# Splitting the last 1 KB of columns off the last store of a 2x2 max-unpool

## Chip, cores, metric

One core of one Trainium2 chip. The metric is device time in microseconds (us) of one execution, as the median of several; "span" is the time from the first to the last instruction in the profile, about 1.3 us shorter. Differences here are a few hundredths to a few tenths of a us in 71.5, so most experiments were timed in five rounds (those with 4 KB columns in three) beside the kernel before, each call on one chip, and the text quotes intervals. SBUF is the memory in which the kernel allocates its tiles, HBM the one that holds its inputs and its output (the profile counts 12.58 MB read from it and 16.78 MB written).

## The reference

```python
# x: 16 x 64 x 32 x 32 float32, indices: int32 in 0..3, kernel_size = 2
for b, c, i, j in every input element:          # loops shortened
    idx = indices[b, c, i, j]
    output[b, c, 2*i + idx // 2, 2*j + idx % 2] = x[b, c, i, j]   # the rest is zero
```

The launch passes the indices as 64-bit integers, so the kernel reads 8.4 MB of indices and 4.2 MB of x, and writes 16.8 MB.

## The kernel before

The 1024 images lie eight to an SBUF row (partition), 128 rows. Four loads are issued at once; VectorE computes each output position as `(index == position) * x`; the output goes out in four stores (NG = 4) of 128 rows x 32 KB. All transfers are issued by SyncE.

```python
        program.first(nc.sync.dma_start(out=x_t, in_=x_v).then_inc(x_in, 16))
        ...                                                   # three loads of idx, VectorE work
        for g in range(NG):
            nc.sync.wait_ge(made, g + 1)
            nc.sync.dma_start(out=out_v[g], in_=out_t[g]).then_inc(
                stored if g else stored_0, 16
            )
        nc.sync.sem_inc(made, -NG)
        program.last(
            nc.sync.wait_ge(stored, 16 * (NG - 1)).then_inc(stored, -16 * (NG - 1))
        )
```

The kernel ends when the last wait sees every increment of the last three stores: in the profile the last of them lands at 70.31 us and the span ends at 70.35.

Of the kernel before, what the change touches and what calls it, by code (L numbers as in the profile page):

```python
# [1 line left out]

# [4 lines left out]

P = 128
F32 = mybir.dt.float32
I32 = mybir.dt.int32  # L10


class Program:




    def __init__(self, nc):
        self.nc = nc
        self.block = nc.main_func.blocks[0]  # L20
        self.kernel_block = nc.cur_bb.bb.name

    def __enter__(self):
        ins = self.block.instructions
        self.branches = [i for i in ins if "Branch" in type(i).__name__]
        n = len(ins) - len(self.branches)
        assert all("Branch" in type(ins[k]).__name__ for k in range(n, len(ins)))
        del ins[n:]
        self.nc.switch_bb(self.block.name, parent=None)
        self.symbolic = self.nc._always_lower_symbolic_ap  # L30
        self.nc._always_lower_symbolic_ap = False
        return self

    def first(self, made):
        ins = self.block.instructions
        assert ins[len(ins) - 1].name == made.ins.name
        moved = ins.pop()
        at = next(
            k
            for k, i in enumerate(ins)  # L40
            if i.engine == moved.engine and isinstance(i, mybir.InstDrain)
        )
        ins.insert(at, moved)

    def last(self, made):


        def move(nc):
            ins = self.block.instructions
            at = next(k for k, i in enumerate(ins) if i.name == made.ins.name)  # L50
            nc.main_func.blocks[-1].instructions.append(ins.pop(at))

        self.nc.at_finalize(move)

    def __exit__(self, kind, *_):
        self.nc._always_lower_symbolic_ap = self.symbolic
        if kind is None:
            for b in self.branches:
                self.block.instructions.append(b)
            self.nc.switch_bb(self.kernel_block, parent=None)  # L60


@with_exitstack
def kernel(
    ctx: ExitStack,
    tc: tile.TileContext,
    x: bass.AP,
    indices: bass.AP,
    kernel_size: bass.AP,
    out: bass.AP,  # L70
):
    nc = tc.nc
    assert kernel_size == 2

    B, C, H, W = x.shape
    n_img = B * C
    T = n_img // P
    assert T * P == n_img and C % T == 0

    G = 2  # L80
    NG = T // G
    FIRST = 3
    N = H * W
    x_v = x.rearrange("b (ch t) h w -> (b ch) (t h w)", t=T)
    idx_v = indices.rearrange("b (ch t) h w -> (b ch) (t h w)", t=T).bitcast(I32)
    out_v = out.rearrange("b (ch g t) oh ow -> g (b ch) (t oh ow)", g=NG, t=G)

    x_t = nc.alloc_sbuf_tensor("x_t", [P, T * N], F32).ap()
    idx_t = nc.alloc_sbuf_tensor("idx_t", [P, T * 2 * N], I32).ap()
    out_t = [  # L90
        nc.alloc_sbuf_tensor(f"out_t{g}", [P, G * 4 * N], F32).ap()
        for g in range(NG - 1)
    ]
    out_t.append(out_t[0])

    x_in = nc.alloc_semaphore("x_in")
    idx_in = [nc.alloc_semaphore(f"idx_in{g}") for g in range(2)]
    made = nc.alloc_semaphore("made")
    stored_0 = nc.alloc_semaphore("stored_0")
    stored = nc.alloc_semaphore("stored")  # L100

    x_c = x_t.rearrange("p (t i j) -> p t i j", t=T, j=W)
    idx_c = idx_t.rearrange("p (t i j two) -> p t i j two", t=T, j=W, two=2)[
        :, :, :, :, 0
    ]
    cut = FIRST * 2 * N

    with Program(nc) as program:
        for part in (slice(0, 2 * N), slice(2 * N, cut)):
            program.first(  # L110
                nc.sync.dma_start(out=idx_t[:, part], in_=idx_v[:, part]).then_inc(
                    idx_in[0], 16
                )
            )
        program.first(nc.sync.dma_start(out=x_t, in_=x_v).then_inc(x_in, 16))
        program.first(
            nc.sync.dma_start(out=idx_t[:, cut:], in_=idx_v[:, cut:]).then_inc(
                idx_in[1], 16
            )
        )  # L120

        nc.vector.wait_ge(x_in, 16).then_inc(x_in, -16)
        for t in range(T):
            g, k = t // G, t % G
            if t in (0, FIRST):
                half = int(t == FIRST)
                n_in = 16 if half else 32
                nc.vector.wait_ge(idx_in[half], n_in).then_inc(idx_in[half], -n_in)  # L128


            if k == 1 and t != FIRST and g:
                continue
            n = 1 if k == 1 or t + 1 == FIRST or not g else 2
            if g == NG - 1:
                nc.vector.wait_ge(stored_0, 16).then_inc(stored_0, -16)
            o_c = out_t[g].rearrange(
                "p (m i two j wo) -> p m i two j wo", m=G, two=2, wo=2, j=W
            )

            parts = (slice(0, H // 2), slice(H // 2, H)) if t == 0 else (slice(0, H),)  # L140
            for rows in parts:
                for pidx in range(4):
                    op = nc.vector.scalar_tensor_tensor(  # L143
                        out=o_c[:, k : k + n, rows, pidx // 2, :, pidx % 2],
                        in0=idx_c[:, t : t + n, rows],
                        scalar=pidx,
                        in1=x_c[:, t : t + n, rows],
                        op0=mybir.AluOpType.is_equal,
                        op1=mybir.AluOpType.mult,
                    )  # L150
            if k + n == G:
                op.then_inc(made, 1)

        for g in range(NG):
            nc.sync.wait_ge(made, g + 1)
            nc.sync.dma_start(out=out_v[g], in_=out_t[g]).then_inc(
                stored if g else stored_0, 16
            )
        nc.sync.sem_inc(made, -NG)
        program.last(  # L160
            nc.sync.wait_ge(stored, 16 * (NG - 1)).then_inc(stored, -16 * (NG - 1))
        )


# [1 line left out]
_INS = ['x', 'indices', 'kernel_size']  # L166
_OUTS = [((16, 64, 64, 64), 'float32')]

_NUMBERS = {'kernel_size': 2}


# [26 lines left out]
```

## Time and profile before

| | before |
|---|---|
| median of 3 runs | 71.46 us (71.41 to 71.53) |
| the execution that was profiled | 71.67 us, span 70.3 us |
| VectorE busy | 36.1 us, 51% |
| DMA packets fill | 97.4% of 16 engines |

### The profile page before, as it was taken

The page shows a single profiled execution, that of the slowest core. Times are in us where ns is not written, and L with a number is a line of the kernel's source. Part 1 is how long each engine was busy: PE and PEld are TensorE (multiplying, and loading weights), DVE is VectorE, ACT ScalarE, POOL GpSimd, SP SyncE. Part 2 cuts the span into 40 slices and gives each one's busy share as a digit, 9 for nine tenths or more (in the row PEclk, how much of TensorE's full clock was granted, in tenths as well). Part 3 has the DMA queues.
Part 4 walks back from the last instruction along what each step waited for, and adds up shares of the span by engine and source line. Part 5 has one row for each costly group of instructions (what it writes and reads, how often), then busy time and mean ns, then how long its engine had stood idle before and what let it go on. Part 6 is the DMA issues. An engine that isn't in the chain of part 4 may idle for free.

```text
span 70.3 us, 81 instructions
## 1 busy us (share of the span) xinstructions
DVE 36.1 (51%) x28; POOL 0.2 (0%) x4
## 2 busy tenths in 40 slices
DVE  0000000000089999999999999999999700000000
POOL 1000000000000000000000000000000000000000
DMA  4999996979988999869898998979698989989790
GB/s 84 405 443 438 456 559 298 578 317 540 429 373 373 466 582 443 373 298 540 354 540 354 429 466 373 522 317 578 298 540 354 522 373 410 484 354 540 317 540 37
DMA packets 1152, 29.36 MB, mean 417 GB/s; under 512 B 128, under 2 KB 128, under 8 KB 128
## 3 DMA queue, kind: packets, MB, share of 16 engines
q1 hardware_dynamic: 1152, 29.36, 97.4%
HBM read 12.58 MB, written 16.78 MB: 417 GB/s over the span
## 4 chain that ended last, share of the span: by engine, by line
DVE 45%; DVEq 5%; issue 2%
DVE out_t L143 45%; DVEq L193 5%
## 5 line engine op out<-in xcount | busy, mean ns | idle before, releaser
L143 DVE SCALAR_TENSOR_TENSOR out_t<-idx_t,x_t 128x1024 f32<-128x1024 int32 (+2 forms) x28 | 36.1, 1370 | 19.6 <-DVEq L128 19.6
L179 POOL MEMSET const-bfloat16-1.0<- 128x1 bf16 x1 | 0.1, 102 | 0.0
L179 POOL MEMSET const-uint8-127<- 128x1 uint8 x1 | 0.1, 102 | 0.0
L179 POOL MEMSET const-float32-0.0<- 128x1 f32 x1 | 0.1, 99 | 0.2 <-issue 0.2
L179 POOL MEMSET const-float32-1.0<- 128x1 f32 x1 | 0.1, 99 | 0.0
## 6 DMA issues: line engine op xcount, KB each, us to landing
out_dram<-out_t SPq DMA_DIRECT2D x4, 4096.0 KB, 13.2
idx_t<-in_indices_dram SPq DMA_DIRECT2D x1, 5120.0 KB, 30.1
x_t<-in_x_dram SPq DMA_DIRECT2D x1, 4096.0 KB, 18.5
idx_t<-in_indices_dram SPq DMA_DIRECT2D x1, 2048.0 KB, 9.3
idx_t<-in_indices_dram SPq DMA_DIRECT2D x1, 1024.0 KB, 4.8
```

The lines of the kernel that those rows point to most:

```text
L143: op = nc.vector.scalar_tensor_tensor(out=o_c[:, k : k + n, rows, pidx // 2, :, pidx % 2], in0=idx_c[:, t : t + n, rows], scalar=pidx, in1 ...
L179: nc = _bacc.Bacc("TRN2", target_bir_lowering=False, num_devices=1)
L193: with _tile.TileContext(nc) as tc:
```

## The change

The intent: if one of the 16 DMA engines ends later than the rest, take some of its share of the last store. The store is cut into 31 KB columns for all 128 rows, the last 1 KB of 120 rows, and the last 1 KB of the other 8 rows. The 120 rows fall to 15 engines, eight rows each, and the 8 rows to eight of them, one each; the sixteenth has 8 KB less to move. Here and in the recorded texts "engine 15" is a name for the engine that gets none of the small rows, or none of a store of 120 rows, "0 to 7" for the eight with nine of them and "8 to 14" for the seven with eight.

```diff
+    REST = 256
...
+        rest = slice(G * 4 * N - REST, None)
+        pieces = (
+            (slice(0, P), slice(0, rest.start)),
+            (slice(0, 15 * P // 16), rest),
+            (slice(15 * P // 16, P), rest),
+        )
         for g in range(NG):
             nc.sync.wait_ge(made, g + 1)
-            nc.sync.dma_start(out=out_v[g], in_=out_t[g]).then_inc(
-                stored if g else stored_0, 16
-            )
+            for rows, cols in pieces if g == NG - 1 else ((slice(0, P), slice(None)),):
+                nc.sync.dma_start(
+                    out=out_v[g][rows, cols], in_=out_t[g][rows, cols]
+                ).then_inc(stored if g else stored_0, 16)
...                                    # the last wait counts 16 * (NG - 2 + len(pieces))
```

More of the change, by code (lines that the diff above doesn't have):

```diff
@@ L152 @@
                 op.then_inc(made, 1)
+        rest = slice(G * 4 * N - REST, None)
[4 more added lines that the diff above has]
+        )
         for g in range(NG):
             nc.sync.wait_ge(made, g + 1)
-            nc.sync.dma_start(out=out_v[g], in_=out_t[g]).then_inc(
-                stored if g else stored_0, 16
-            )
+            for rows, cols in pieces if g == NG - 1 else ((slice(0, P), slice(None)),):
+                nc.sync.dma_start(
+                    out=out_v[g][rows, cols], in_=out_t[g][rows, cols]
+                ).then_inc(stored if g else stored_0, 16)
         nc.sync.sem_inc(made, -NG)
-        program.last(
-            nc.sync.wait_ge(stored, 16 * (NG - 1)).then_inc(stored, -16 * (NG - 1))
-        )
+        n_stored = 16 * (NG - 2 + len(pieces))
+        program.last(nc.sync.wait_ge(stored, n_stored).then_inc(stored, -n_stored))
 _INS = ['x', 'indices', 'kernel_size']
```

## The prediction

Where the prediction rests on something that no trace or run here shows, the passage is cut and the cut is marked. The forecast's sum came to a gain of 0.06 us, 71.40 us in all. The split of the small rows over the engines, on which the 300, 46 and 95 ns rest, was taken as given before any run had shown it. And the small case enters at 0.03, the lower end of "0.03 to 0.08", because I supposed that the two next lanes were among those with nine small rows, which was not shown.

> **What bounds the kernel now.** I read the page's slices first, then the queue, then the chain of waits, and last the single packets and landings in the trace.
>
> ```profile
> DVE  0000000000089999999999999999999700000000
> DMA  4999996979988999869898998979698989989790
> DMA packets 1152, 29.36 MB, mean 417 GB/s; under 512 B 128, under 2 KB 128, under 8 KB 128
> q1 hardware_dynamic: 1152, 29.36, 97.4%
> ```
>
> In the 40 slices the DMA row is full from the second slice to the last but one; VectorE works only in the middle. The queue line says that packets fill 97.4% of the time of 16 engines. Of 1152 packets 1024 are rows (128 rows by 8 transfers) and 128 are small: 8 transfers by 16 engines, each engine's increment of the completion counter. Then the same by stretches (stretch and its length, busy VectorE, busy GpSimd, granted clock, DMA share, GB/s):
>
> ```profile
> 2.00:20.00 18.00, 0.36 (x1) 0.00 (x0) 1.00 1.02 436
> 20.00:45.00 25.00, 25.00 (x24) 0.00 (x0) 1.00 1.00 432
> 55.00:66.00 11.00, 0.79 (x1) 0.00 (x0) 1.00 1.02 441
> ```
>
> Loads, mixed part and stores all move 432 to 441 GB/s: there is no hole for a better order to fill. The chain that ended last names VectorE for 45%, but it ends at 44.78 + 11.01 = 55.8 us, where the fourth store is issued; the last 14.5 us are that store's time from issue to landing:
>
> ```profile
> 41.48 3.30 DVEq L193
> 44.78 11.01 DVE out_t L143 x5
> ```
>
> ```profile
> L156 SPq DMA_DIRECT2D out_dram<-out_t x4: 332/338/348, 29.1 to 55.8; - x4
> DMA to landing us min/median/max: 12.1/13.2/14.5
> ```
>
> The reader should see here that the store is issued (0.34 us of the issuing queue) long before the engines come to it: the third store lands only at 60.6 us. VectorE could be some 3 us later at no cost (an estimate: the engines take the fourth store up at 60.1, it is issued at 55.8, and at the start 1 us passed from issue to first packet). So the end is set by the DMA engines, and of these by the one that lands last.
>
> The trace has each packet. Following end to start, they fall into 16 unbroken lanes of 72 packets. In a lane a row of 8 KB takes 306 ns, of 16 KB 607, of 32 KB 1209.3, of 40 KB 1510.5, and the small packet about 6. A line through these: 4.9 ns + bytes x 0.03676 ns (27.2 bytes per ns; 16 engines give 435 GB/s, as seen). All lanes run at this same pace; they differ by when they started. Their first packets begin between 1.02 and 1.92 us and take 307 to 1282 ns; by the end the lanes' last small packets lie between 69.24 and 69.84 us, and the 16 landings of the last store at 69.57 (first), ..., 69.97 (thirteenth), 70.12, 70.18 and 70.31 us. Then SyncE passes its last wait and the span ends at 70.35. The last lane to finish is also the last to start (1.92 us; it loses another 0.12 us on the way, 0.08 of it at 56.4), and the two before it are ones whose first packet was slow (1195 and 1282 ns) though they began at 1.02 and 1.03. The records carry no engine numbers, so which engine is the last lane is my inference.
>
> [...]
>
> **The change, part by part.** No VectorE instruction moves; the comparison of instructions shows only the last store replaced by three: 128 rows of 31 KB, 120 rows of 1 KB, 8 rows of 1 KB. The bytes are the same.
> - Issue: two more, 2 x 0.34 = 0.68 us on the queue, from 55.8 to about 56.8. Engines come to the first piece at about 60.1 us and to the small ones at about 69. Hidden; cost 0.
> - Now, last store, every engine: 8 x 1209.3 + 6 = 9680 ns.
> - Engine 15 after: 8 x (4.9 + 31744 x 0.03676) + 6 = 8 x 1171.8 + 6 = 9380 ns, 300 less.
> - Engines 8 to 14: 9380 + 8 x (4.9 + 1024 x 0.03676) + 6 = 9380 + 8 x 42.5 + 6 = 9726, 46 more.
> - Engines 0 to 7: one more row and increment, 9726 + 42.5 + 6 = 9775, 95 more.
> - The end. If engine 15 is the last lane, it lands at 70.31 - 0.30 = 70.01 and no longer counts. The next, 70.18, becomes 70.18 + 0.05 to 0.10 = 70.23 to 70.28. Gain: 0.03 to 0.08 us.[...]
> - The spread at the start is drawn anew each time. The change is sized as if engine 15 ran 0.3 us behind all others, a size someone must have seen; were the two slow first packets absent, the next lane is at 69.97 and the end at 70.02 to 70.07, a gain of 0.25 to 0.30. That is the most the idea can give. I weigh the small case about three to one over the large: 0.75 x 0.03 + 0.25 x 0.25 = 0.085, less a little for the rivals below, so 0.06: 71.46 - 0.06 = 71.40 us.
>
> **The rivals.**
> 1. Engine 15 is not the last lane, or not by more than the 46 to 95 ns put on the others. Then the last lane merely carries more: 70.31 + 0.05 to 0.10, time 71.51 to 71.56. For it: no engine number in the records, and two lanes only 0.13 and 0.19 behind the last one. Against it: the last lane differs from the others by starting alone, 0.29 us after the fifteenth[...].
> 2. A 1 KB row costs more than the line says. At 70 ns, say, instead of 42.5, eight rows add 220 ns, and the end is 0.15 to 0.2 later than in the sum: about 71.6. For it: no row below 8 KB in the trace, and all small rows go out in the same third of a microsecond to addresses 128 KB apart[...]. Against it: increments pass at 6 ns, so an engine can step from packet to packet that fast, and first-load rows of 8 KB[...] keep to the line.
> 3. The three-piece wait ends later by itself: a new fixed cost between pieces. Against it: at each transfer border of a lane there is only the 6 ns increment, and the landing follows it by 0.33 to 0.47 us in any case. Expected 0.
> 4. Issue becomes the limit. It would need about 12 us of slack to vanish; I give this next to nothing.
>
> **Range and chances.** What can move is bounded by a few hundred ns: best case -0.30, rival 2 in strength +0.3. The three times before lie between 71.41 and 71.53, so noise of medians is some 0.05. Eight times in ten I expect 71.22 to 71.58. Two per cent is 1.43 us, nearly five times the largest effect in the sum[...]. Faster by 2%: 0.005; within: 0.985; slower: 0.01.
>
> **What will show it.** In the changed trace: 1024 + 128 = 1152 row packets (128 of them of 1 KB), 16 x 8 + 15 + 8 = 151 increments, 1303 in all; the issuing line 6 times; and VectorE unchanged at 36.1 us. Right: 1 KB packets spaced about 42 ns, one lane with no 1 KB packet, ending about 0.35 us earlier against the others than an unrelieved lane would, and a span of 70.0 to 70.3 us. Wrong: the relieved lane lies in the middle of the field (rival 1), packets of 1 KB spaced 60 ns and more (rival 2), a gap before the small pieces in the lanes (3 and 4), or a lane with other than 0, 8 or 9 small rows[...].

## The result

| | before | after |
|---|---|---|
| median (6 runs each, same rounds) | 71.50 us (71.41 to 71.55) | 71.68 us (71.64 to 71.83) |
| ratio | | 1.0030, 95% interval 1.0017 to 1.0043 |
| the profiled execution | 71.67 us, span 70.3 | 71.83 us, span 70.5 |

Slower by 0.2 us: within 2%, but outside the predicted range of 71.22 to 71.58 and on the other side of zero. Ratios here are the mean time of one kernel's fast runs over that of the other's of the same rounds, so not quite the ratio of the medians that are quoted.

The page of the changed kernel, slices and queue:

```profile
DVE  0000000000089999999999999999999600000000
DMA  5999996979988999869697999989796979898982
DMA packets 1303, 29.36 MB, mean 416 GB/s; under 512 B 151, under 2 KB 279, under 8 KB 279
q1 hardware_dynamic: 1303, 29.36, 97.4%
```

The packet counts are the predicted ones: 1303 in all, 151 increments, 279 - 151 = 128 rows of 1 KB. VectorE is unchanged. The issuing line (instructions, and shortest, median and longest time in ns):

```profile
L166 SPq DMA_DIRECT2D out_dram<-out_t x6: 332/346/1337, 29.1 to 57.5; - x6
```

The two small pieces took 1.34 and 1.20 us to issue, not 0.34 as predicted. The last is through at 58.7 us, still 10 us before the engines come to it, and no lane has a gap there; so that miss costs nothing. (Nor is 0.34 right for the four loads at the start, also issued back to back: 0.4 to 0.7 us each.) Stretches (columns as in the prediction):

```profile
2.00:20.00 18.00, 0.41 (x1) 0.00 (x0) 1.00 1.01 435
20.00:45.00 25.00, 25.00 (x24) 0.00 (x0) 1.00 1.00 434
55.00:66.00 11.00, 0.74 (x1) 0.00 (x0) 1.00 1.03 444
```

The same rates as before, so it is the end that has to be looked at, a few tenths of a us that no share of busy time shows. There the packets give, with the 16 lanes (taken as one DMA engine's packets each) followed as in the prediction:

- Rows of 1 KB are spaced 42 to 43 ns, as the line through the larger rows said (42.5).
- Eight lanes have nine of them, seven have eight, one has none: the split that the prediction counted on. The lane with none is the one called engine 15.
- The lane with none is not the last one. By the end of its 31 KB rows it is twelfth or thirteenth of 16, 0.12 us before the last.
- The last increment is sent at 69.85 us, as in the profile before (69.84). It lands at 70.47, after 0.62 us; before, 0.47.

### The profile page after: what moved, and what is told of

Same layout as the page of the kernel before. It is cut to its first block, busy times and chain, and to the rows that moved or that the text cites. A ratio compares the mean times of both kernels' runs of the same rounds, so it can differ in the third digit from the quotient of the medians.

```text
span 70.5 us, 83 instructions
## 1 busy us (share of the span) xinstructions
DVE 36.1 (51%) x28; POOL 0.2 (0%) x4
## 2 busy tenths in 40 slices
DMA packets 1303, 29.36 MB, mean 416 GB/s; under 512 B 151, under 2 KB 279, under 8 KB 279
## 3 DMA queue, kind: packets, MB, share of 16 engines
q1 hardware_dynamic: 1303, 29.36, 97.4%
## 4 chain that ended last, share of the span: by engine, by line
DVE 45%; DVEq 5%; issue 2%
DVE out_t L144 45%; DVEq L202 5%
```

## The experiments

Kernels not marked as wrong gave correct results. "Over" and "under" are against the kernel before. The three theories, as named in the expectations: **W**, only packet work counts (46 ns on engines 8 to 14, 95 on 0 to 7); **L**, landing takes longer behind small rows; **P**, how long a row takes depends on which SBUF rows the transfer reads. P came up only after the fourth run. P's figures are my estimates.

**Small pieces first.** The three pieces in another order.

```diff
         pieces = (
-            (slice(0, P), slice(0, rest.start)),
             (slice(0, 15 * P // 16), rest),
             (slice(15 * P // 16, P), rest),
+            (slice(0, P), slice(0, rest.start)),
         )
```

> Same three pieces, but the two small ones are issued ahead of the big one, so the same rows fall to the same engines while the last things written are 31 KB rows and 16 increments. Theory W (packet work: engine 15 is not the last, and the others carry 46 to 95 ns more): the same as the changed kernel, about 0.18 us over the kernel before (71.68 against 71.50). Theory L (landing: after its last small rows an engine's increment takes some 0.15 us longer to land, 620 instead of 471 ns in the two profiles): 0.10 to 0.15 us less than the changed kernel, that is 0.03 to 0.08 over the kernel before.

Correct; 71.55 us, ratio 1.0012 (0.9998 to 1.0026), 0.04 over by medians and 0.09 by the ratio. Between the two theories and clear of neither: inconclusive.

**The small piece over all 16 engines.**

```diff
-            (slice(0, 15 * P // 16), rest),
-            (slice(15 * P // 16, P), rest),
+            (slice(0, P), rest),
```

> The last 1 KB of columns as one transfer of 128 rows over all 16 engines: no engine is relieved, every engine has 8 small packets and one increment more. W: plus 46 ns over the kernel before (+0.05 us). L: plus 46 ns and most of the longer landing, +0.15 to +0.2 us, like the changed kernel. If engine 15 was the last and its relief counted, this one is slower than the changed kernel by up to 0.3 us.

Correct; 71.55 against 71.51, ratio 1.0002 (0.9989 to 1.0016). Small rows at the end of the kernel, and one increment more on every engine, cost 0.01 to 0.04 us, in keeping with W's 46 ns (the interval goes up to 0.11). L as stated is refuted: its last increment landed after 0.38 us. And a kernel that relieves nobody has the lower ratio, 1.0002 against the changed kernel's 1.0030. They were run at other times.

**Without the piece of 8 rows** (wrong: those 8 KB are not written; the third line of `pieces` is deleted).

> Wrong on purpose: without the transfer of 8 small rows. Engines 0 to 14 have 8 small rows each. W: 0.05 us less than the changed kernel (one packet and one increment, 48 ns, less on engines 0 to 7), if one of these is the last; else the same. L: 0.05 to 0.15 less, if it is the third piece that lands late.

71.64 us, ratio 1.0017 (1.0005 to 1.0029): 0.13 over, 0.04 under the changed kernel's 71.68. It was run at another time.

**Engine 15 without work in the last store** (wrong: rows 120 to 127 are not written).

```diff
-            (slice(0, P), slice(0, rest.start)),
-            (slice(0, 15 * P // 16), rest),
-            (slice(15 * P // 16, P), rest),
+            (slice(0, 15 * P // 16), slice(None)),
```

> Wrong on purpose: the last store writes 120 rows of 32 KB only (15 engines, 8 rows each), rows 120 to 127 of it are never written. Engine 15 has no work in the last store and there are no small rows. If engine 15 sets the end of the kernel before, this is faster by 0.1 us or more (0.13 by the gap of its last two landings, up to 0.3). If it is not the last (rival 1), there is no change: within 0.03 us of the kernel before.

80.77 us: 9.3 us *over*, with less to write. Neither theory had that. The stretch from 62 to 68 us of this kernel (length, VectorE, GpSimd, clock, DMA share, GB/s):

```profile
62.00:68.00 6.00, 0.00 (x0) 0.00 (x0) 1.00 0.82 180
```

and of the kernel before:

```profile
62.00:68.00 6.00, 0.00 (x0) 0.00 (x0) 1.00 1.00 431
```

The engines are as busy as their packets are long, and move less than half. In the packets a 32 KB row takes about 2549 ns on 14 engines and 1213 on one. The stores of 128 rows take about 1213 ns a row on all 16 lanes. So a row of 32 KB can take twice as long in one transfer as in another, and this trace doesn't say why. My guess was the source side: that it depends on which SBUF rows the transfer reads. That is theory P, tested next.

**The same 120 rows, read from other SBUF rows** (wrong in its values).

The source is 15 SBUF rows 9 apart, each read eight times. In the following, `dst` is `out_v[g]` and `src` is `out_t[g]`, and each pair is one transfer.

```diff
-            (slice(0, 15 * P // 16), slice(None)),      # dst[0:120] <- src[0:120]
+  (dst[0:120].rearrange("(a b) c -> a b c", b=8),
+   src[0:127:9].unsqueeze(1).broadcast_to([15, 8, 4 * G * N])),
```

> Wrong on purpose: as the kernel that left out rows 120 to 127 (80.77 us; 32 KB rows of 2549 ns on 14 engines and 1213 on one), with the same 120 destination rows[...]. [...]P: all 15 engines keep 1210 ns per row. Rival Q (a split over 15 engines is slow by itself, or it is the HBM side): again 2549 ns and 80.8 us. If the first, this is also the clean test of engine 15: time equal to before within 0.05 us if engine 15 is not always the last, 0.13 us or more less if it is.

71.53 against 71.51, ratio 1.0004 (0.9989 to 1.0020); all 120 rows at 1213 ns. The stretch:

```profile
62.00:68.00 6.00, 0.00 (x0) 0.00 (x0) 1.00 0.95 410
```

15/16 of 435 GB/s would be 408. So P holds for rows of 32 KB: with the destinations, the number of engines and the packets unchanged, other source rows take the row from 2549 to 1213 ns. That one row is now read eight times is a second difference; the runs with 8 rows of 4 KB, below, have none of that and show the like (213 to 441 against 159 ns). And this is the clean test of the change's idea: engine 15 has *nothing* to do for the last ten us, and the kernel ends no earlier. By the interval a gain of more than 0.08 us is excluded; one of 0.03 is not. But the trace shows who is last. Engine 15's lane finished the third store at 60.09 us, fifteenth of 16, and did nothing after that. The last increment of all is sent at 69.89 us, 0.24 us after the one before it, by another lane. A straggler as large as the one that the change was to relieve is there with engine 15 idle.

**88 rows** (wrong; the last store is rows 0 to 87 only).

> Wrong on purpose: the last store writes rows 0 to 87 in full rows (11 engines, 8 rows each). P: [...]8 engines at about 2549 ns a row and 3 at 1213, end like the 120 rows, near 80.8 us. Q: all 11 alike.

80.62 us in one look. Of the rows that begin between 61 and 68 us, 18 take 1.2 us and 24 take 2.3 to 2.8 us: three engines with six rows each, and eight engines with three. P's count, not Q's.

**The small rows from two sets of SBUF rows.** The 120 x 1 KB piece alone, read from SBUF rows 9 or 8 apart (both wrong).

```diff
-            (slice(0, 15 * P // 16), rest),
-            (slice(15 * P // 16, P), rest),
+  (dst[0:120, rest].rearrange("(a b) c -> a b c", b=8),
+   src[0:127:9, 0:2048].rearrange("p (b c) -> p b c", b=8)),     # the other kernel: src[0:113:8, 0:2048]
```

> Wrong on purpose: the big piece and the 120 x 1 KB piece as in the run without the third piece (71.64 us, 0.13 over before), same packets, engines and destinations, but the small rows are read from SBUF rows 0, 9, ..., 126[...]. P: the 0.13 us goes, to within 0.05 us of the kernel before (packet work +46 ns on 15 engines, engine 15 relieved). Otherwise (W or L): as without the third piece, +0.1 to +0.15 us.

> Wrong on purpose: the same with SBUF rows 0, 8, ..., 112[...]. P: +0.1 to +0.15 us over the kernel before, as in the run without the third piece[...].

P expected 0.1 us between the two, the other theories nothing. Both 71.55 against 71.51; ratios 1.0004 (0.9991 to 1.0018) and 1.0010 (0.9996 to 1.0025). No difference that the times can tell. The packets settle it: from either set all 120 small rows took 46 ns, and so did all 128 in the first trace of the changed kernel. No row of 1 KB was slowed there, which that first trace could already have told.

**Four times the columns.** REST = 1024, first all three pieces (correct), then without the last (wrong).

P's sum in the first expectation and P's figures in the second are my estimates from the 155 ns of a 4 KB row (by the line through the larger rows): at most eight such rows more, 1.2 us, for the piece of 120 rows, and four, 0.6 us, for the piece of 8.

> The changed kernel with four times the columns split off (4 KB rows instead of 1 KB; a correct kernel). W (work only): engines 0 to 14 carry 8 x 4.9 + 6 = 45 ns more and engines 0 to 7 another 155 + 6, so about +0.2 us over the kernel before. [...]Sum for P: +0.5 to +1.8 us, with 4 KB packets longer than 155 ns in the trace.

> Wrong on purpose: the same without the piece of 8 rows. W: +0.05 us or less. P: +0.3 to +1.2 us; the difference to the previous run is the price of the piece of 8 rows: W 0.16, P 0.3 to 0.6.

71.87 us, ratio 1.0048 (1.0026 to 1.0070), 0.36 over; and 71.59, ratio 1.0006 (0.9988 to 1.0024), 0.08 over. In both traces 91 of the 4 KB rows take 159 ns and the rest up to 0.44 us (first kernel) and 0.39 (second), so some rows are slowed here; but the end is far from P's half a us and more. The piece of 8 rows costs 71.87 - 71.59 = 0.28 us, where W says 0.16.

**The piece of 8 rows alone**, 4 KB of rows 120 to 127 (wrong), then the same read from SBUF rows 4 apart: `src[120:, rest]` becomes `src[0:29:4, rest]`. P's 600 ns, in the first expectation, is again four rows of 155 ns.

> Wrong on purpose: 28 KB of each row over 16 engines and then only the piece of 8 rows of 4 KB (rows 120 to 127[...]). Relative to the kernel before, the 16 engines save 8 x (1209.3 - 1058.9) = 1203 ns; then W: plus 155 + 6, that is -1.04 us; P: plus up to 600, -0.6 to -0.8 us.

> Wrong on purpose: as the run before, the 8 rows of 4 KB read from SBUF rows 0, 4, ..., 28 instead[...]. Both theories: -1.04 us. P has it 0.2 to 0.4 us faster than with rows 120 to 127, W equal.

70.35 and 70.45 us: 1.16 and 1.06 under. The packets agree with P: from rows 120 to 127 two of the eight take 159 ns and six 213 to 441, and from rows 4 apart all eight take 159. The time does not: the kernel with the slow rows is if anything the faster. In its trace the last 4 KB row ends at 68.546 us and the last 28 KB row, on another lane, at 68.549: the slow rows were just hidden. With this P is dropped as the cause of the 0.2 us.

At this point twelve kernels had run, relieving engine 15 was known to gain nothing, and open were the size of the cost and the straggler that I had seen in the first profile.

**Both kernels again, and the changed kernel with other source rows** at 1 KB: unaltered copies; the last piece's source as just above; both pieces' sources as above.

> The changed kernel again, unaltered. It is to say how much of its +0.18 us is steady and how much is the draw: in its profile (71.83, the slowest of its six times) the last increment took 620 ns to land, in eight other runs 331 to 411. Expected: ratio 1.002 to 1.004 again, +0.15 to +0.25 us, and a last landing lag of some 350 to 450 ns in a typical execution. If it comes out under 1.001, the first measurement was itself a draw.

> The kernel before again, unaltered, against itself: ratio 1.000 within 0.0015. Its profile is a second draw of the lanes: the first was of an execution of 71.67 us, 0.2 over the median, and its last lane ended at 69.84 with a landing lag of 471 ns. If that was an unlucky draw (my new theory D: the straggler that the change was to relieve is not there in a typical execution), this one ends at 70.05 to 70.2 us with its last two lanes within 0.1 us and a lag under 420. If the straggler is steady: 70.3 us and a gap of 0.13 us again.

> Wrong on purpose: the changed kernel, with the 8 rows of 1 KB of its last piece read from SBUF rows 0, 4, ..., 28[...] and not from rows 120 to 127[...]. W: as the changed kernel. P for the last piece: 0.05 to 0.1 us less than the changed kernel.

> Wrong on purpose: both small pieces read[...] (rows 9 apart, and 4 apart). Same packets, engines and destinations as the changed kernel. W: as the changed kernel. P: only the packet work is left, +0.05 to +0.1 us over the kernel before, 0.1 us less than the changed kernel of the same call.

| kernel | median us | ratio to before (71.47) | 95% interval |
|---|---|---|---|
| before again | 71.47 | 0.9997 | 0.9983 to 1.0011 |
| changed again | 71.64 | 1.0018 | 1.0004 to 1.0032 |
| last piece from other rows | 71.66 | 1.0022 | 1.0007 to 1.0038 |
| both small pieces from other rows | 71.65 | 1.0020 | 1.0006 to 1.0035 |

The cost is steady, 0.17 us by medians, and in these times the source rows have no part in it. The second profile of the kernel before begins with these lines of its page:

```profile
span 70.1 us, 81 instructions
## 1 busy us (share of the span) xinstructions
DVE 36.1 (52%) x28; POOL 0.2 (0%) x4
```

against

```profile
span 70.3 us, 81 instructions
```

for the first. Same kernel, same rates (438 GB/s from 55 to 66 us, 441 in the first), 0.25 us between them: 70.10 and 70.35. In the second the last four increments are sent at 69.56, 69.59, 69.64 and 69.69 us and the last lands after 0.38 us, at 70.07. The straggler of the first profile (69.84, landing 70.31) is not there. Theory D (the straggler belongs to that one slow execution) holds, for the two executions seen.

## Why the prediction was wrong

**What bounds the kernel: right.** DMA engines at full rate to the end; VectorE and the issue had room. The issue was mis-sized (1.34 and 1.20 us, not 0.34 each) and stayed hidden.

**Packet work: right.** Rows of 1 KB at 42 to 43 ns; nine, eight and no small rows; 46 and 95 ns more. Rival 2 fell: all 16 engines writing small rows last cost 0.01 to 0.04 us (interval up to 0.11).

**"If engine 15 is the last lane, it lands at 70.31 - 0.30 = 70.01 and no longer counts": this step failed.** I took a gain of 0.03 us at three to one over 0.25. No gain is measured: with engine 15 idle through the whole last store the ratio is 1.0004 (0.9989 to 1.0020), which excludes the large case (0.25 to 0.30 us) and leaves room for no more than 0.08; and another lane was last by 0.24 us in that run. Three things were wrong in it.

- I read the straggler off one profile whose execution took 71.67 us, 0.2 over the median of 71.46. Both numbers were before me. A profile of a typical execution (71.43 us) has the last lane 0.15 us earlier, and its landing lag is 0.38 and not 0.47. Subtracting a straggler's excess from the *median* counted a delay that the median does not contain. It was a mistake of kind, not of size: the excess of a slow draw can't be earned.
- The reason given for engine 15 as the last lane, that the last lane to finish is the one that started last (1.92 us), can't be read from the trace. That lane and one that began at 1.02 us with a first packet of 1195 ns run 13 ns apart until 31 us. Then the second loses 13 ns, and from 33 to 40 us the two lie within 2 ns of each other. Which of them loses the later 0.12 us and ends last, the records don't say.
- The idea isn't baseless: with 1 KB rows the relieved lane can be told apart in most traces, and engine 15 is a late one: last by 0.18 us in the run with source rows 8 apart, fifteenth of 16 in four others (no third piece, source rows 9 apart, both small pieces from other rows, changed again; 0.01 to 0.11 us before the last; in changed again it may as well be the last), twelfth or thirteenth in the first profile of the changed kernel, about tenth with the small pieces first. But in these some other lane ends within about 0.2 us of it or after it, and that one is not relieved; it is loaded.

**Rival 1 is what happened**, "the last lane merely carries more". I had it at 71.51 to 71.56 us; measured were 71.68 and 71.64. Four kernels with three pieces (changed twice, last piece from other rows, both from other rows) have ratios of 1.0030, 1.0018, 1.0022 and 1.0020, on average 1.0022, that is +0.16 us. Four with one small piece of 1 KB at the end (over 16 engines, no third piece, source rows 9 apart and 8 apart) have 1.0002, 1.0017, 1.0004 and 1.0010, on average 1.0008, +0.06 us, where the sum had 0.046. So the first 0.06 is accounted for. (Small pieces first, with three pieces in another order, is in neither group: 1.0012.) The piece of 8 rows costs about 0.10, where the sum had 0.048, and at 4 KB it cost 0.28, where the sum had 0.16.

**What stays open.** Where the other 0.05 us of the last piece comes from. It is no larger than the half-width of one interval (0.0013 x 71.5 = 0.09), so it may not exist. Its own source rows are ruled out as far as the times tell (71.66 us with other rows, 71.64 without). In the three-piece kernels the median lag from the sending of an increment of the last store to its landing (the n-th sent paired with the n-th landed) is 405 to 415 ns, in the others with 1 KB rows last, and before, 369 to 387. For the last eight increments alone it is 449 to 469 ns against 361 to 381, which is 0.07 to 0.11 us, about what is missing. So a longer landing behind the piece of 8 rows, a narrower form of L, is not excluded and was not tested; against it, the three pieces with 4 KB rows have 375 ns there and an excess as well. The two profiles of the exact changed kernel have a last lag of 620 and 562 ns, those with the last piece or both pieces from other rows 421 and 364, though their times are alike. With one trace each I don't read more into it. Nor did I learn which other engine is as late as 15.

No version beats the kernel before: the bytes are fixed, every lane is full from its first packet to its last (no gap in the traces of both kernels, packets fill 97.4%), and all that differs is where the lanes stand: by some 0.6 us in the first profile of the kernel before, with the last at 69.84 us, and otherwise in the second, with the last at 69.69. None was tried beyond those above.

## What to carry to other kernels

Before you earn a gap that one profile shows at the end of a kernel, check that the profiled execution is a typical one, and take a second profile: here the last of the 16 lanes ended at 69.84 us in one and at 69.69 in the other. Shaving one engine while loading fifteen gains only if that engine is the last by more than the load, in most executions. Test such an idea by removing the whole of the suspect's work, free of side effects; if that gains nothing, no redistribution will. And look at the packet times of a DMA over another number of rows before you trust its bandwidth: here a store of 120 rows of 32 KB ran at 2549 ns a row on 14 engines, where 128 rows ran at 1213 on 16.
